# Recurrent gates on two 64-row halves of the matrix array, and a written order for the recurrence

## The chip, the cores and the metric

The kernel runs on one core of a Trainium2 chip. A core has a matrix engine (TensorE, PE in the rows; its weight loads are PEld), a vector engine (VectorE, DVE), a scalar engine (ScalarE, ACT), a general engine (GpSimd, POOL) and a queue engine that issues most DMAs (SyncE, SP). The metric is the device time of one execution in microseconds (us), the median of three runs.

## The reference

Two layers of a latent-diffusion backbone, on 256 context and 1024 latent tokens of width 1024 (T = 1280 in the kernel). The change lies in layer 0, where one projection `z = u @ w_in` feeds a bidirectional gated recurrence (16 heads of 64 channels), a Fourier mixer and a SiLU gate path. What the gates compute:

```python
xh = xc.reshape(b_, length, LRU_HEADS, LRU_HEAD_DIM)          # 16 heads x 64
g = einsum('blhi,ghij->gblhj', xh, gate_w) + gate_b           # g: recurrence gate, input gate
r = sigmoid(g[0]); i = sigmoid(g[1])
log_a = -LRU_C * r * softplus(-lam)
a = exp(log_a)
b = sqrt(-expm1(2 * log_a)) * (i * xc)                        # then h_t = a_t h_(t-1) + b_t
```

There are two directions, so four 64x64 gate matrices per head; `xc` is a depthwise convolution of width 4 of the recurrent part of z. Both scans are added and multiplied by `silu` of the gate path. The Fourier mixer takes four other groups of 128 channels of z, and layer 1 is a latent attention, which the change leaves alone.

## The kernel before, in words

Channels lie on partitions, tokens along the free axis. The projection is computed in 24 blocks of 128 output channels: `in0(m)` (lines 259 to 272) fills `z_m` in PSUM from 8 k-tiles in 3 passes (high weight by high input, high by low, low by high: an exact split of float32 in two), each pass in pieces of 512, 512 and 256 tokens. One such pass of three matmuls is called a position below; a block has 24. Blocks 0 to 7 are the recurrent channels (tile j holds heads 2j and 2j+1), 8 to 11 the Fourier groups (`fourier`, line 434), 12 to 19 the gate paths of tiles 0 to 7. Two blocks of z have room in PSUM, beside two banks (`gtile`, line 141) for everything else. The blocks run in the order z12, z0, z1, z2, z13, z3, z14, ..., z7, z18, z19, z8, z9, and so on.

`w0_load` (line 274) brings a block's weights (512 KB) and splits them: DVE makes the high part, POOL the low part (line 82), in two rotating buffers. `conv` (line 310) reads z with one ACT pass (bias) and six DVE passes (the taps, line 317), loads and splits the gate weights, and splits `xc`. The gate weights are a block-diagonal 128x128 matrix for each of the four gates of a tile. `gate_units` (line 332) makes 12 units of a tile: direction, gate and piece; each is three matmuls of 128 rows (`mm3`, lines 85 to 87) into one bank, and one ACT sigmoid over 128 partitions (line 345). `lru_chain` (line 349) is what follows on a tile: tanh and exp on ACT (354, 357), the drive on POOL (359), squares and square roots on ACT (361, 364), the DVE products (362, 367) and scans (369 to 379), the sum of directions on POOL (381), and the product with the gate path on DVE (402), whose result is written out.

The adaptive-norm weights of layer 1 and of the output gates are worked in between: `ada_units` (line 169) makes 16 units, each a load of 1 MB into the one `adaw` buffer, eight rows of matmuls of 32 columns (line 166), and a DVE addition out of PSUM (line 181).

The units are placed as small pieces of work between the k-tiles of `in0` (`spread`, line 255), so that the gates of tile j stand in z_(j+1), those of tile 7 in z19. The order on each engine is chosen by a scheduler from dependences; where a buffer must come free first, the instruction waits for it. SP issues its DMAs in one order, and one that waits holds those behind it. The Fourier stage's buffers (`ft_p`, line 411) take the place of those of the recurrence, so its first copy `fu<-z` (line 443) waits for the last product of tile 7 (line 402); block z10 needs the PSUM that this copy frees.

Of the kernel before, what the change touches and what calls it, by code (L numbers as in the profile page):

```python
# [38 lines left out]
PD = {0: 8, 1: 8}  # L39
# [15 lines left out]
def _body(ctx, tc, ap, out, dbg=None):  # L55
# [113 lines left out]
    def ada_units(src, row, nm):  # L169

        us = []
        for kt in range(KT):
            def u(kt=kt):
                w = aw_p.tile([P, 2048], F32, tag="adaw", name=f"adaw{nm}{kt}")
                load(w, src[kt])
# [6 lines left out]
            us.append(u)  # L182
# [26 lines left out]
    ada_end = {}  # L209

# [38 lines left out]
    ada_work = ada_units(ap["ada_1"], row1, "m") + [lambda: ada_mod(1, row1)]  # L249
    ada_work += ada_units(ap["ada_g"], rowg, "g") + [lambda: ada_gate(rowg)]  # L250
# [8 lines left out]
    def in0(m, work=()):  # L259
        wh, wl = ws.pop(m) if m in ws else w0_load(m)  # L260
        z = z_ps.tile([P, 1536], F32, tag="z", name=f"z{m}")
        for kt in range(KT):

            with tc.issue_after(ada_end[IA[m, kt]]) if (m, kt) in IA else ExitStack():
                for wi, ui in ((wh, uh), (wh, ul), (wl, uh)):
                    for a, n in CH3:
                        TE.matmul(z[:, a : a + n], wi[:, kt, :], ui[kt][:, a : a + n],  # L267
                                  start=(kt == 0 and ui is uh and wi is wh),
                                  stop=(kt == KT - 1 and wi is wl))
            for u in spread(work, KT, kt):  # L270
# [39 lines left out]
    def conv(j, work=()):  # L310
        z = in0(j, work)
        xc = lru.tile([P, T], F32, tag="xc", bufs=2, name=f"xc{j}")
        S.activation(out=xc, in_=z[:, :T], func=AF.Identity, scale=vv("convw", 4 * j + 1), bias=vv("convb", j))
        for k in (0, 2, 3):
            for s, e in ((0, NC), (NC, T)):
                lo, hi = max(s, s + 1 - k), min(e, e + 1 - k)
                V.scalar_tensor_tensor(out=xc[:, lo:hi], in0=z[:, lo + k - 1 : hi + k - 1],  # L317
                                       scalar=vv("convw", 4 * j + k), in1=xc[:, lo:hi], op0=ALU.mult, op1=ALU.add)
        gw = lru.tile([P, 4, P], F32, tag="gw", name=f"gw{j}")
        load(gw, ap["gw"][j])  # L320
        gh = lru.tile([P, 4, P], F32R, tag="gh", name=f"gh{j}")
        gl = lru.tile([P, 4, P], F32R, tag="gl", name=f"gl{j}")
        split(gh, gl, gw, V, G)
# [1063 lines left out]
```

## Time and profile before

| | us |
| --- | --- |
| median of three runs | 1456.05 (1453.4 to 1458.35) |
| the profiled execution's own time | 1450.71 |
| its span | 1448.9 |
| PE busy | 1402.8 (97%) |
| DVE busy | 903.4 (62%) |
| POOL busy | 678.5 (47%) |
| ACT busy | 541.3 (37%) |

The mean granted clock of the matrix engine in this execution was 0.995 of full speed. The chain of work that ended last is for 73% PE and for 17% DVE.

How to read the rows further down. A row of the timeline gives the start in us from the span's start, the duration in us, the engine, the line, the operation, its operands (out<-in, buffer numbers left out), its shapes and how many followed in a run (x3); in brackets at the end the idle time before it and what ended that. Matmuls overlap, so what one costs is read from the starts, not from the durations. A row of the windows gives the stretch, its length, then for PE, PEld, DVE, ACT and POOL the busy us with the number of instructions, then the granted clock of PE (1.00 is 2.4 GHz, 0.50 is 1.2 GHz), the mean busy share of the DMA engines, and GB/s. A row of the waits gives the waiting engine, name and line, what it waited for, then us in total, times, and the longest.

### The profile page before, as it was taken

What the parts mean: (1) busy time and instruction counts of PE and PEld (TensorE: products, weight loads), DVE (VectorE), ACT (ScalarE), POOL (GpSimd) and SP (SyncE); (2) the same over time, 40 slices, a digit from 0 to 9 for tenths busy, and PEclk for the clock granted to TensorE, in tenths of its full rate; (3) what the DMA queues carried; (4) which work ended last, traced back from release to release, by engine and by line L of the source; (5) the groups of instructions that cost most, each with busy time, mean ns of one, the idle gap of its engine ahead of it and who ended that gap; (6) DMA issues with size and microseconds to landing.
All of it is one profiled execution on the core that took longest, in us unless ns stands there. A gap on an engine that the chain in (4) does not pass through costs nothing.

```text
span 1448.9 us, 19809 instructions
## 1 busy us (share of the span) xinstructions
PE 1402.8 (97%) x7912; PEld 1005.8 (69%) x7912; DVE 903.4 (62%) x1454; ACT 541.3 (37%) x664; POOL 678.5 (47%) x314
## 2 busy tenths in 40 slices
PE   6998999999999999998999999999999999999997
PEld 3776777777788878887986665555555555555686
DVE  5659768665855343336835446657565757563798
ACT  2276666656112231103431143344434344445210
POOL 1124434444210233312241158667766876699643
PEclk9999999999999999999999999999999999999999
DMA  8713232233303473321061131011101010124342
GB/s 301 248 52 113 98 113 102 95 105 106 126 16 97 157 248 119 115 71 34 34 182 66 44 99 51 23 45 48 52 16 38 29 38 16 37 69 167 115 131 88
DMA packets 65869, 134.10 MB, mean 93 GB/s; under 512 B 5864, under 2 KB 31720, under 8 KB 63472
## 3 DMA queue, kind: packets, MB, share of 16 engines
q1 hardware_dynamic: 63328, 124.83, 26.3%
q0 software_dynamic: 2016, 7.60, 1.4%
q8 instruction: 62, 1.02, 0.3%
q10 hardware_dynamic: 432, 0.39, 0.1%
q14 instruction: 31, 0.25, 0.1%
HBM read 101.14 MB, written 24.66 MB: 87 GB/s over the span
## 4 chain that ended last, share of the span: by engine, by line
PE 73%; DVE 17%; issue 3%; DMA 3%; ACT 2%; POOL 1%; SPq 0%; DVEq 0%; POOLq 0%; ACTq 0%
PE s L1073 13%; PE z L267 11%; PE y L646 10%; PE po L1089 10%; PE mx L976 6%; PE in1g L85 2%; PE in1g L87 2%; PE in1g L86 2%; DVE xc L317 2%; PE yf L1210 2%; DVE gate L367 1%; DVE th L362 1%; DVE hf L1260 1%; DVE gate L378 1%; PE rp L1106 1%
## 5 line engine op out<-in xcount | busy, mean ns | idle before, releaser
L1079 POOL TENSOR_TENSOR ra<-ra,p 128x1024 f32<-128x1024 f32 x112 | 269.9, 2410 | 90.2 <-ACT p L1075 87.0
L978 DVE TENSOR_REDUCE m<-mx 128x1 f32<-128x512 f32 (+1 forms) x384 | 210.3, 590 | 100.4 <-PE mx L976 99.5
L1075 ACT ACTIVATE p<-s 128x1024 f32<-128x1024 f32 x160 | 163.5, 1026 | 203.9 <-PE s L1073 202.0
L267 PE MATMUL z<-uh,w0h 128*128 128x512 f32 (+1 forms) x576 | 149.8, 367 | 4.3 <-ACT uh L76 4.3
L82 POOL TENSOR_TENSOR w0l<-w,w0h 128x1024 fp32r<-128x1024 f32 x24 | 63.9, 2664 | 184.0 <-DVE w0h L78 127.8
L267 PE MATMUL z<-ul,w0h 128*128 128x512 f32 (+1 forms) x576 | 148.0, 362 | 0.0
L267 PE MATMUL z<-uh,w0l 128*128 128x512 f32 (+1 forms) x576 | 147.8, 362 | 0.0
L267 PEld LDWEIGHTS z<-uh,w0h 128*128 128x128 f32 x576 | 98.1, 190 | 33.3 <-issue 10.7
L267 PEld LDWEIGHTS z<-ul,w0h 128*128 128x128 f32 x576 | 97.0, 191 | 18.8 <-issue 1.2
L267 PEld LDWEIGHTS z<-uh,w0l 128*128 128x128 f32 x576 | 96.5, 190 | 18.4 <-issue 2.0
L1073 PE MATMUL s<-R,KR 33*128 33x512 f32 (+1 forms) x640 | 101.4, 392 | 0.0
L345 ACT ACTIVATE gate<-gps,vec 128x512 f32<-128x512 f32 (+1 forms) x96 | 57.6, 617 | 103.2 <-PE gps L87 103.1
L976 PEld LDWEIGHTS mx<-Kh,Qh 64*128 64x128 f32 x384 | 38.3, 185 | 65.3 <-DVE m L978 31.3
L976 PE MATMUL mx<-Kh,Qh 64*128 64x512 f32 (+1 forms) x384 | 81.9, 404 | 1.3 <-DVE m L978 1.3
L1089 PE MATMUL po<-p,v_even 128*64 128x512 f32 x320 | 77.5, 605 | 0.0
L1089 PE MATMUL po<-p,v_odd 128*64 128x512 f32 x320 | 77.5, 605 | 0.0
L381 POOL TENSOR_TENSOR gate<-gate,gate 128x1280 f32<-128x1280 f32 x8 | 23.9, 2992 | 112.2 <-DVE gate L378 97.1
L976 PE MATMUL mx<-KR,R 64*128 64x512 f32 (+1 forms) x384 | 71.6, 355 | 0.0
L1073 PEld LDWEIGHTS s<-R,KR 33*128 33x128 f32 (+1 forms) x640 | 61.0, 184 | 13.4
L1073 PE MATMUL s<-Qh,Kh 64*128 64x512 f32 x320 | 69.8, 431 | 0.0
L649 DVE TENSOR_TENSOR n<-gbc,y 128x1024 f32<-128x1024 f32 x10 | 12.2, 1222 | 85.7 <-PE y L646 85.7
L1114 DVE RECIPROCAL ri<-ri 128x128 f32<-128x128 f32 x64 | 59.4, 938 | 9.9 <-ACT ri L1109 9.9
(358 smaller groups left out, 3063.0 us busy)
## 6 DMA issues: line engine op xcount, KB each, us to landing
w<-in_w SPq DMA_DIRECT2D x24, 512.0 KB
adaw<-in_ada SPq DMA_DIRECT2D x32, 256.0 KB
adawm<-in_ada SPq DMA_DIRECT2D x8, 1024.0 KB
adawg<-in_ada_g SPq DMA_DIRECT2D x8, 1024.0 KB
y_dr<-sg SPq DMA_DIRECT2D x10, 640.0 KB
woraw<-in_wo SPq DMA_DIRECT2D x12, 512.0 KB
xt<-in_x_cm SPq DMA_DIRECT2D x8, 640.0 KB
yra<-y_dr SPq DMA_DIRECT2D x10, 512.0 KB
```

What stands on the lines that cost most here:

```text
L82: el.tensor_tensor(out=lo, in0=src, in1=f(hi), op=ALU.subtract)
L85: TE.matmul(o, lh, rh, start=start, stop=False)
L267: TE.matmul(z[:, a : a + n], wi[:, kt, :], ui[kt][:, a : a + n], start=(kt == 0 and ui is uh and wi is wh), stop=(kt == KT - 1 and wi is wl))
L345: S.activation(out=gt[d, g][:, a : a + n], in_=ps[:, :n], func=AF.Sigmoid, bias=vv("gateb", 4 * j + i))
L646: TE.matmul(ps[:, 512 * hf : 512 * hf + 512], a[k], b[k][:, 512 * hf : 512 * hf + 512], start=(k == 0 and a is yh and b is woh), stop=(k = ...
L976: TE.matmul(ps[a][:, :n], q[r, P * t : P * t + P], k[r, a0 : a0 + n], start=st, stop=not st)
L978: V.tensor_reduce(out=m3s[t][:, a, i : i + 1], in_=ps[a][:, :n], axis=AX.X, op=ALU.max)
L1073: TE.matmul(ps[:, a, :], k[r, ks], w[r, c], start=(j == 0), stop=(j == len(parts) - 1))
L1075: S.activation(out=es, in_=ps, func=AF.Exp, scale=SCALE)
L1079: G.tensor_tensor(out=ra, in0=st["e"][0] if kt == 1 else ra, in1=es, op=ALU.add)
L1089: TE.matmul(st["o"][64 * a : 64 * a + 64, :], quad[q][6][:, k, 128 * i + 64 * a : 128 * i + 64 * a + 64], st["e"][k][:, a, :], start=(k == ...
L1114: V.reciprocal(out=st["ri"][:, d], in_=st["ri"][:, d])
```

## The change

The gate weights are stored as 128x2x128: row halves are the two heads of the tile, and the 128 columns of a direction hold the 64 outputs of both gates. A unit is now a direction and a piece: for each of the three passes, two matmuls of 64 rows, head 0 on the upper half of the array's rows and head 1 on the lower, each into a bank of its own (line 375 of the new kernel). Its result is read by four sigmoids over 64 partitions (line 379): two heads by two gates. A tile so has 6 units of 6 matmuls and 24 sigmoids. The gate weight load shrinks from 256 to 128 KB, and its splits by half. The scans write into another buffer.

From z1 to the end of z8, PE, DVE, ACT and POOL issue what the code writes, in the order in which it is written; SP's order is still chosen. Per tile there are 48 positions (z_(j+1), then z_(13+j)), and `slots0` says what is issued after which. The blocks now run z12, z0, z1, z13, z2, z14, ..., z7, z19, z8, z9, and the gates of tile 7 stand in z8. An adaptive-norm unit stands at positions 0, 38 and 44 of each tile, and its load is issued after the unit before it.

```diff
+            def dma(kt=kt):
+                adaw[nm, kt] = aw_p.tile([P, 2048], F32, tag="adaw", name=f"adaw{nm}{kt}")
+                load(adaw[nm, kt], src[kt])
             def u(kt=kt):
-                w = aw_p.tile([P, 2048], F32, tag="adaw", name=f"adaw{nm}{kt}")
-                load(w, src[kt])
+                w = adaw.pop((nm, kt))
                 acc = gtile(f"ada{nm}{kt}")
...
-            us.append(u)
+            us.append((dma, u))
...
-    def in0(m, work=()):
+    def in0(m, work=(), at=None):
         wh, wl = ws.pop(m) if m in ws else w0_load(m)
         z = z_ps.tile([P, 1536], F32, tag="z", name=f"z{m}")
         for kt in range(KT):
             with tc.issue_after(ada_end[IA[m, kt]]) if (m, kt) in IA else ExitStack():
-                for wi, ui in ((wh, uh), (wh, ul), (wl, uh)):
+                for i, (wi, ui) in enumerate(((wh, uh), (wh, ul), (wl, uh))):
                     for a, n in CH3:
                         TE.matmul(z[:, a : a + n], wi[:, kt, :], ui[kt][:, a : a + n],
                                   start=(kt == 0 and ui is uh and wi is wh),
                                   stop=(kt == KT - 1 and wi is wl))
+                    for u in at.get(3 * kt + i, ()) if at else ():
+                        u()
...
-        gw = lru.tile([P, 4, P], F32, tag="gw", name=f"gw{j}")
...
+        gws[j] = lru.tile([P, 2, P], F32, tag="gw", name=f"gw{j}")
...
+    def gates(j, d, c):
+        def run():
+            a, n = CH3[c]
+            if c == 0:
+                for g in range(2):
+                    gt[j, d, g] = lt(f"gate{d}{g}_{j}")
+            gh, gl = gws[j]
+            xh, xl = hls[j]
+            ps = [gtile(f"gps{j}{d}{c}{h}") for h in range(2)]
+            for i, (w, x) in enumerate(((gh, xh), (gh, xl), (gl, xh))):
+                for h in range(2):
+                    r = slice(64 * h, 64 * h + 64)
+                    TE.matmul(ps[h][:, :n], w[r, d, :], x[r, a : a + n], start=(i == 0), stop=(i == 2))
+            for h in range(2):
+                for g in range(2):
+                    r = slice(64 * g, 64 * g + 64)
+                    S.activation(out=gt[j, d, g][64 * h : 64 * h + 64, a : a + n], in_=ps[h][r, :n], func=AF.Sigmoid,
+                                 bias=vv("gateb", 4 * j + 2 * h + d)[r, :])
+        return run
...
-                        mm3(ps[:, :n], gh[:, i, :], gl[:, i, :], xh[:, a : a + n], xl[:, a : a + n], True, True)
-                        S.activation(out=gt[d, g][:, a : a + n], in_=ps[:, :n], func=AF.Sigmoid, bias=vv("gateb", 4 * j + i))
...
+    order0.enter_context(tc.manual_schedule(engines={e.engine for e in (TE, V, S, G)}))
+    def ada_next():
+        if ada_work:
+            _, u = ada_work.pop(0)
+            u()
+        if ada_work and ada_work[0][0]:
+            ada_work[0][0]()
...
+        c, b = ch[j], ch.get(j - 1)
+        A, B, nxt = j + 1, 13 + j, j + 2 if j < 6 else 8
+        if j < 7:
+            put_(0, ada_next, lambda: w0_dma(nxt), lambda: gw_dma(A))
+            put_(4, lambda: w0_high(B), lambda: w0_low(B))
+        if b:
+            put_(0, b["square", 1])
+            put_(1, b["beta", 0])
+            put_(2, b["root", 0])
+            put_(3, b["beta", 1])
+            put_(4, b["root", 1])
+            put_(5, b["scaled", 0], b["scan", 0])
+            put_(6, b["scaled", 1], b["scan", 1])
+            put_(7, lambda: silu(j, 0))
+            put_(11, lambda: silu(j, 1))
+            put_(12, b["both"])
+            put_(21, b["gated"])
+        us = [gates(j, d, k) for d in range(2) for k in range(3)]
+        for p, u in zip(UNITS[0 if j == 0 else 1 if j < 7 else 2], us):
+            put_(p, u)
+        if j == 7:
+            return w
+        put_(25 if j == 0 else 21, c["drive", 0])
+        put_(24, lambda: conv_bias(A))
+        put_(25, lambda: conv_taps(A, CUTS[:2]))
+        put_(28, lambda: conv_taps(A, CUTS[2:]))
+        if j < 6:
+            put_(24, lambda: w0_dma(B + 1))
+        put_(30, lambda: w0_high(nxt), lambda: w0_low(nxt))
+        put_(35, c["drive", 1], lambda: x_split(A, 0), lambda: x_split(A, 1), lambda: gw_split(A))
+        put_(38, ada_next)
+        put_(44, ada_next)
+        put_(36, c["tanh", 0], c["tanh", 1])
+        put_(39, c["exp", 0])
+        put_(42, c["exp", 1])
+        put_(46, c["square", 0])
+        return w
+    UNITS = ((16, 21, 24, 27, 31, 34), (10, 15, 20, 23, 29, 34), (8, 12, 15, 17, 20, 23))
+    for j in range(7):
+        w = slots0(j)
+        zc[j + 1] = in0(j + 1, at={p: w[p] for p in range(24)})
+        zc[13 + j] = in0(13 + j, at={p: w[24 + p] for p in range(24)})
+    z8 = in0(8, at=slots0(7))
+    order0.close()
...
-            gw[j, s, :, s] = lru_gate_w[0].reshape(4, H, 64, 64)[:, 2 * j + h].transpose(1, 0, 2)
+    a["gw"] = lru_gate_w[0].reshape(2, 2, 8, 2, 64, 64).transpose(2, 3, 4, 0, 1, 5).reshape(8, P, 2, P)
```

On PE, one gate unit of tile 3 in block z4. In the names, `gps3000` is the gates' PSUM tile of tile 3, `xh3`, `xl3` the split input, `gh3`, `gl3` the split gate weights, `z4` the block, `uh`, `ul`, `w0h`, `w0l` its operands. Before:

```order
L267 MATMUL z4_1392<-uh0_120,w0l_4_1389 128x512 x2
L267 MATMUL z4_1392<-uh0_120,w0l_4_1389 128x256
L85 MATMUL gps3000_1403<-xh3_1267,gh3_1263 128x512
L86 MATMUL gps3000_1403<-xl3_1268,gh3_1263 128x512
L87 MATMUL gps3000_1403<-xh3_1267,gl3_1264 128x512
L267 MATMUL z4_1392<-uh1_121,w0h_4_1388 128x512 x2
L267 MATMUL z4_1392<-uh1_121,w0h_4_1388 128x256
```

And now:

```order
L270 MATMUL z4_1523<-ul3_131,w0h_4_1422 128x512 x2
L270 MATMUL z4_1523<-ul3_131,w0h_4_1422 128x256
L375 MATMUL gps3000_1588<-xh3_1454,gh3_1458 128x512
L375 MATMUL gps3001_1589<-xh3_1454,gh3_1458 128x512
L375 MATMUL gps3000_1588<-xl3_1455,gh3_1458 128x512
L375 MATMUL gps3001_1589<-xl3_1455,gh3_1458 128x512
L375 MATMUL gps3000_1588<-xh3_1454,gl3_1459 128x512
L375 MATMUL gps3001_1589<-xh3_1454,gl3_1459 128x512
L270 MATMUL z4_1523<-uh3_123,w0l_4_1423 128x512 x2
```

The unit of three matmuls into one bank is one of six into two, and stands further back in its block.

On SP, the DMAs issued around tiles 1 to 3 with what each waits for (`Pool`: POOL's semaphore, `PE`: PE's; `DMAHW`: an earlier transfer). `adawm5` is the load of the sixth adaptive-norm unit, `w0_4` the weights of block 4, `gw3` gate weights, `y_dr` a result written out. Before:

```order
L61 DMA adawm3_1089<-in_ada_1 128x2048 [waits DMAHW6_49,DMAHW1_49,PE_49]
L61 DMA y_dr_150<-sg0_522 128x1280 [waits DVE_49]
L61 DMA gw3_1261<-in_gw 128x512 [waits DMAHW0_49,Pool_49]
L61 DMA w0_4_1386<-in_w0 128x1024 [waits DMAHW5_49,Pool_49]
L61 DMA adawm4_1206<-in_ada_1 128x2048 [waits DMAHW1_49,PE_49]
L61 DMA w0_15_1578<-in_w0 128x1024 [waits DMAHW7_49,Pool_49]
L61 DMA y_dr_150<-sg1_1097 128x1280 [waits DVE_49]
L61 DMA adawm5_1373<-in_ada_1 128x2048 [waits DMAHW5_49,PE_49]
```

And now:

```order
L60 DMA adawm3_903<-in_ada_1 128x2048 [waits DMAHW1_49,DMAHW0_49,PE_49]
L60 DMA adawm4_925<-in_ada_1 128x2048 [waits DMAHW1_49,PE_49]
L60 DMA w0_15_1080<-in_w0 128x1024 [waits DMAHW5_49,Pool_49]
L60 DMA y_dr_150<-sg0_522 128x1280 [waits DVE_49]
L60 DMA w0_4_1231<-in_w0 128x1024 [waits DMAHW6_49,Pool_49]
L60 DMA adawm5_1177<-in_ada_1 128x2048 [waits DMAHW2_49,PE_49]
L60 DMA gw3_1233<-in_gw 128x256 [waits DMAHW7_49,Pool_49]
L60 DMA adawm6_1207<-in_ada_1 128x2048 [waits DMAHW6_49,PE_49]
L60 DMA adawm7_1229<-in_ada_1 128x2048 [waits DMAHW0_49,PE_49]
```

The adaptive-norm loads, which stood one by one among the others, now stand in twos and threes, and `adawm5` stands right behind `w0_4`.

On PE at the end of the stretch, where block z9 ends and the Fourier stage's first products (`dft_c`, `dft_s`, then `aps0a`, `aps0b` from the folded copy `fold`) stand. Before:

```order
L267 MATMUL z9_2877<-uh7_127,w0l_9_2874 128x512 x2
L267 MATMUL z9_2877<-uh7_127,w0l_9_2874 128x256
L440 MATMUL dft_c_2837<-fw_2738,cosd_2740 128x512
L440 MATMUL dft_s_2840<-fw_2738,sind_2741 128x512
L267 MATMUL z10_3051<-uh0_120,w0h_10_3047 128x512 x2
L267 MATMUL z10_3051<-uh0_120,w0h_10_3047 128x256
L267 MATMUL z10_3051<-ul0_128,w0h_10_3047 128x512 x2
L267 MATMUL z10_3051<-ul0_128,w0h_10_3047 128x256
L267 MATMUL z10_3051<-uh0_120,w0l_10_3048 128x512 x2
L481 MATMUL aps0a_2905<-cw_100,fold_2737 128x128 x4
```

And now:

```order
L270 MATMUL z9_2976<-uh7_127,w0l_9_2973 128x512 x2
L270 MATMUL z9_2976<-uh7_127,w0l_9_2973 128x256
L564 MATMUL dft_c_2936<-fw_2916,cosd_2918 128x512
L564 MATMUL dft_s_2939<-fw_2916,sind_2919 128x512
L605 MATMUL aps0a_3004<-cw_100,fold_2915 128x128 x4
L605 MATMUL aps0b_3022<-sw_101,fold_2915 128x128 x4
L270 MATMUL z10_3150<-uh0_120,w0h_10_3146 128x512 x2
```

The eight matmuls of z10 that stood ahead of `aps0a` stand behind it.

## Rows read from the trace of the kernel before

**Rows 1.** The windows, the stretch of the recurrence.

```profile
160.00:365.00 205.00, 200.14 (x1045) 158.81 (x1044) 147.17 (x129) 130.23 (x136) 82.32 (x31) 1.00 0.30 101
```

**Rows 2.** The timeline of PE, two positions of a block.

```profile
78.57 0.75 PE L267 MATMUL z<-uh,w0h 128*128 128x512 f32 x3
79.16 0.75 PE L267 MATMUL z<-ul,w0h 128*128 128x512 f32 x3
```

**Rows 3.** The timeline of PE in layer 1, 64-row among 128-row matmuls.

```profile
804.34 0.39 PE L87 MATMUL in1g<-u1h,wgl 128*128 128x512 f32 x1
804.66 0.49 PE L976 MATMUL mx<-Kh,Qh 64*128 64x512 f32 x2
805.00 0.40 PE L976 MATMUL mx<-KR,R 64*128 64x512 f32 x2
805.32 0.50 PE L85 MATMUL in1g<-u1h,wgh 128*128 128x512 f32 x1
805.66 0.40 PE L86 MATMUL in1g<-u1l,wgh 128*128 128x512 f32 x1
```

**Rows 4.** The waits of PE, 57 to 365 us.

```profile
PE gps L85 <- DVE adarow L181: 6.3, 3, 4.0
PE gps L85 <- DVE adarowg L181: 3.2, 3, 1.1
PE gps L85 <- DVE mod L191: 1.2, 1, 1.2
```

**Rows 5.** The timeline of PE, then of SP: an adaptive-norm unit and the next load.

```profile
228.54 1.06 PE L166 MATMUL adag<-adawg,cond 128*32 128x512 f32 x8
...
229.66 0.33 SPq L61 DMA_DIRECT2D adawg<-in_ada_g  x1
```

**Rows 6.** The windows behind that load.

```profile
231.00:234.00 3.00, 3.00 (x17) 2.56 (x16) 0.20 (x1) 1.83 (x3) 0.00 (x0) 1.00 0.83 341
234.00:237.00 3.00, 3.00 (x19) 2.56 (x18) 2.15 (x2) 3.00 (x5) 2.27 (x1) 1.00 0.00 0
```

**Rows 7.** The timeline of ACT, the gates and the chain of tile 7.

```profile
347.87 0.68 ACT L345 ACTIVATE gate<-gps,vec 128x512 f32<-128x512 f32 x1
348.44 1.35 ACT L354 ACTIVATE th<-gate,vpos 128x1280 f32<-128x1280 f32 x1
349.69 0.47 ACT L345 ACTIVATE gate<-gps,vec 128x256 f32<-128x256 f32 x1
...
351.47 1.37 ACT L357 ACTIVATE aa<-gate,vneg 128x1280 f32<-128x1280 f32 x1
357.98 2.42 ACT L361 ACTIVATE gate<-aa 128x1280 f32<-128x1280 f32 x2
```

**Rows 8.** The timeline of DVE (taps), and a group of the page (POOL's splits).

```profile
237.34 4.82 DVE L317 SCALAR_TENSOR_TENSOR xc<-z,vec,xc 128x255 f32<-128x255 f32 x6
...
L82 POOL TENSOR_TENSOR w0l<-w,w0h 128x1024 fp32r<-128x1024 f32 x24 | 63.9, 2664 | 184.0 <-DVE w0h L78 127.8
```

**Rows 9.** The timeline of PE, DVE and ACT: end of z8, of tile 7, Fourier's start.

```profile
366.85 0.39 PE L267 MATMUL z<-uh,w0h 128*128 128x512 f32 x1
...
380.93 1.02 PE L440 MATMUL dft_c<-fw,cosd 128*128 128x512 f32 x2
...
386.64 0.57 PE L481 MATMUL aps0a<-cw,fold 128*128 128x128 f32 x3 [2.21 <-DVE fold L458]
...
375.43 3.67 DVE L402 TENSOR_TENSOR sg<-sg,gate 128x1280 f32<-128x1280 f32 x1 [2.85 <-POOL gate L381]
...
379.21 1.23 ACT L443 COPY fu<-z 128x1280 f32<-128x1280 f32 x1 [15.07 <-DVE fold L459]
```

**Rows 10.** The windows at two waits of PE.

```profile
113.00:117.40 4.40, 0.38 (x3) 0.03 (x1) 4.40 (x3) 1.94 (x2) 2.38 (x1) 0.86 0.55 225
117.40:120.00 2.60, 2.60 (x8) 2.23 (x9) 2.60 (x4) 0.69 (x1) 0.00 (x0) 0.50 0.63 252
385.00:388.00 3.00, 1.36 (x12) 1.39 (x13) 3.00 (x12) 0.19 (x1) 0.00 (x0) 1.00 1.09 399
```

More of the change, by code (lines that the diff above doesn't have):

```diff
@@ L38 @@
 CUT = (0, 1)
-PD = {0: 8, 1: 8}
 ORD = "a0 w0 u0 u1 a1 w1 u2 u3 a2 u4 u5 a3 u6 u7"
@@ L209, in _body @@
     ada_end = {}
+    adaw = {}
     def ada_part(h):
@@ L272, in in0, with w0_dma, w0_high, w0_low @@
         return z
-    def w0_load(m, eh=V):
-        w = w_p.tile([P, KT, P], F32, tag="w", name=f"w0_{m}")
-        load(w, ap["w0"][m])
+    wr = {}
+    def w0_dma(m):
+        wr[m] = w_p.tile([P, KT, P], F32, tag="w", name=f"w0_{m}")
+        load(wr[m], ap["w0"][m])
+    def w0_high(m, eh=V):
         wh = w_p.tile([P, KT, P], F32R, tag="wh", name=f"w0h_{m}")
         wl = w_p.tile([P, KT, P], F32R, tag="wl", name=f"w0l_{m}")
-        split(wh, wl, w, eh, G)
-        return wh, wl
+        copy(eh, wh, wr[m])
+        ws[m] = wh, wl
+    def w0_low(m):
+        wh, wl = ws[m]
+        G.tensor_tensor(out=wl, in0=wr.pop(m), in1=f(wh), op=ALU.subtract)
+    def w0_load(m, eh=V):
+        w0_dma(m)
+        w0_high(m, eh)
+        w0_low(m)
+        return ws[m]
     ws = {}
@@ L308, in _body @@
     lru, lru_c = pool("lru", side="right")
[L310 to L318, printed above, removed]
-        gw = lru.tile([P, 4, P], F32, tag="gw", name=f"gw{j}")
[L320 to L323, printed above, removed]
-        xh = lru.tile([P, T], F32R, tag="xh", name=f"xh{j}")
-        xl = lru.tile([P, T], F32R, tag="xl", name=f"xl{j}")
-        split(xh, xl, xc, V, V)
-        return xc, gh, gl, xh, xl
+    CUTS = [(k, max(lo, lo + 1 - k), min(e, e + 1 - k)) for k in (0, 2, 3) for lo, e in ((0, NC), (NC, T))]
@@ new lines, in gw_dma, with gw_split, x_split @@
+    def gw_dma(j):
+        gws[j] = lru.tile([P, 2, P], F32, tag="gw", name=f"gw{j}")
+        load(gws[j], ap["gw"][j])
+    def gw_split(j):
+        gh = lru.tile([P, 2, P], F32R, tag="gh", name=f"gh{j}")
+        gl = lru.tile([P, 2, P], F32R, tag="gl", name=f"gl{j}")
+        split(gh, gl, gws[j], V, G)
+        gws[j] = gh, gl
+    def x_split(j, part):
+        if part == 0:
+            hls[j] = [lru.tile([P, T], F32R, tag=f"x{c}", name=f"x{c}{j}") for c in "hl"]
+            V.tensor_copy(out=hls[j][0], in_=xcs[j])
+        else:
+            V.tensor_tensor(out=hls[j][1], in0=xcs[j], in1=f(hls[j][0]), op=ALU.subtract)
@@ new lines, in silu @@
+    def silu(j, part):
+        if part == 0:
+            sgs_[j] = lru.tile([P, T], F32, tag="sg", bufs=2, name=f"sg{j}")
+            S.activation(out=sgs_[j], in_=zc[12 + j][:, :T], func=AF.Sigmoid)
+        else:
+            V.tensor_tensor(out=sgs_[j], in0=sgs_[j], in1=zc[12 + j][:, :T], op=ALU.mult)
+    zc[12] = in0(12)
+    silu(0, 0)
+    silu(0, 1)
+    zc[0] = in0(0)
+    conv_bias(0)
+    conv_taps(0, CUTS)
+    gw_dma(0)
+    gw_split(0)
+    x_split(0, 0)
+    x_split(0, 1)
+    w0_load(1)
@@ new lines, in _body @@
+    UNITS = ((16, 21, 24, 27, 31, 34), (10, 15, 20, 23, 29, 34), (8, 12, 15, 17, 20, 23))
[5 more added lines that the diff above has]
+    order0.close()
+    c = ch[7]
+    for n in ("drive", "tanh", "exp", "square", "beta", "root", "scaled", "scan"):
+        for d in range(2):
+            c[n, d]()
+    c["both"]()
+    c["gated"]()
@@ L434, in fourier @@
     def fourier(g, work=()):
-        z = in0(8 + g, work)
+        z = in0(8 + g, work) if g else z8
         if g == 0:
```

136 lines of the change are left out of this document (61 added, 75 removed).

## The prediction

> **What bounds the kernel now.** I read the windows first. Over the stretch that the change touches PE is busy 200.1 of 205 us at the full clock, ACT 130, DVE 147, POOL 82 [rows 1]: PE sets the time, and what is taken from or added to its work counts in full, until another engine's chain is late. Next the waits of PE in this stretch: three entries, 6.3, 3.2 and 1.2 us, 10.7 in all, named as gate matmuls waiting for the additions of adaptive-norm units in the two PSUM banks [rows 4]; those additions waited for loads. Last the timeline at the end of the stretch, where the recurrence hands over to the Fourier stage: z8 ends at 366.85, z9 and the two small transforms run beside the last tile's chain, and PE waits only 2.2 us for the folded copy [rows 9]. So before, work of PE covers that chain nearly to its end.
>
> **The gates themselves.** Consecutive positions start .59 apart [rows 2], for 1280 columns, so a 512-column matmul takes .235 and a 256-column one .117. A tile's gates before: 8 units of 3 x .235 and 4 of 3 x .117, 7.05 us. Now 6 units a tile. The nearest rows for two 64-row matmuls among 128-row ones are in layer 1 [rows 3]: from the start at 804.34 to that at 805.66 stand a 128-row matmul, two pairs of 64-row ones and a 128-row one, four slots of .235, .94, and they take 1.32. Two pairs start .34 + .32 apart where the halves one after another would take .94: the halves do run side by side, and leaving and re-entering the 128-row form costs about .38 in all. A unit then costs 3 x .235 + .38 = 1.09, or .73 for 256 columns; a tile 4 x 1.09 + 2 x .73 = 5.82. Gain 1.23 x 8 tiles: **-9.8**. Bounds: if the change of form cost nothing, -28.2; if the halves ran one after another with that price, +18 more than before.
>
> The Trainium skill speaks to this place on both sides, in "TensorEngine Tiling (Array Packing)": its section Theoretical Speedup gives up to 2x for a contraction of 64 or less, by which alone this term would be -28.2; its section Key Properties says that changing the tiling mode drains the engine. The trace agrees with the second, .38 for an excursion [rows 3].
>
> **The adaptive-norm loads.** The 10.7 us of waits go, since the units stand elsewhere. What is late next: a unit's 8 matmuls take 1.06, and the next load, with one buffer, is issued 1.12 after the unit's start [rows 5]. Its traffic is over by 234.0 [rows 6], 4.3 us at most after the issue at 229.66. So two units can't start closer than about 5.4. From position 44 to position 0 of the next tile PE has 1.06 + 4 x .587 = 3.4: it waits 2.0, in four tiles (the 18 pieces of work, mod and gate among them, last for six tiles; where the pair is broken by those two, no load is needed): 8. From 38 to 44 it has 1.06 + 6 x .587 = 4.6, a wait of .85 if the load leaves at once. But SP holds it behind the next block's weights, which wait for POOL's low split (the place shown in the order, `adawm5` behind `w0_4`). That split is reached from the end of z through sigmoids queued on ACT (4 x .57 = 2.3), the bias pass (1.3) [rows 7], the taps (4.8), the high part (about 1, my estimate from the low part's 2.66) and the low part (2.66) [rows 8]: 12.1 us, then the 512 KB of weights go ahead of or beside the load, half its bytes. PE is through the unit at position 38 after 15 x .587 + 1.8 of gates + 1.06 = 11.7. So the load leaves some .4 late and lands 1.3 later for the shared traffic: a wait of 2.5, in three tiles, 7.5; in tile 0, where the load stands behind gate weights that wait for POOL's second drive, I take 4.5. Together 20, less 10.7: **+9.3**. Bounds: none of these waits, -10.7; each 2 us longer, +25.
>
> **ACT's sigmoids.** A 64-partition sigmoid isn't in the trace. The nearest row is the 128-partition one, .57 for 512 columns from start to start [rows 7], and I take the same, since the columns are as many; half of that is the lower bound. A unit then holds ACT for 2.3 (1.4 for 256 columns), and both banks with it, while PE comes back to the gates after three positions (1.76) at five places in tiles 0 and 7: .5 each, 2.5. In z8 the sigmoids also queue behind what is left of tile 6 on ACT (a square, two roots, a SiLU pass at about 1.25 and two or three table loads of 1.3, some 8 us from the block's start [rows 7]), where the first unit's results are ready at 5.8: another 2.5. **+5**; bounds 0 and, with ACT late in every tile, +40. In tiles 1 to 6 the gaps are five positions behind 512-column units: hidden. ACT would then have some 30 us of work in a tile of 37.
>
> **The end of the stretch.** Before, the last sigmoid of tile 7 ends at 350.16, during z19, and `aps0a` starts at 386.64: 36.5 [rows 7, 9], with z8, z9 and two transforms to cover it. Now tile 7's gates stand in z8, one block later, and only z9 (366.85 to 380.93, 14.1) and the transforms (1.0) come before `aps0a`, for z10 needs the PSUM that the copy frees. The chain itself: 36.5, less some 4 in which the SiLU pass of tile 7 stood in it (the first exp ends about 352.7, a second would end at 354, the squares start at 357.98), plus 1.25 for a tanh that now follows the last sigmoid, 33.7; from the last gate matmul to the last sigmoid's end 1.5. So the last gate matmul to `aps0a` takes 35, where the end of z8 to `aps0a` took 386.64 - 366.85 = 19.8: **+15**. Bounds: +12 if nothing else of the Fourier setup delays the chain (no excess in the 33.7 taken from a shared stretch), +19 if the 4 us don't go.
>
> **The clock.** In the wait of 4.4 at 113 the granted clock falls to the lower level and stays there for some us of work behind it (.86, then .50); in a stretch with 1.6 us of idle time at 385 it stays at 1.00 [rows 10]. So waits of 2 to 4 us can cost about as much again, or nothing. Before lost some 5 us so by its two longest waits (an estimate from the windows at .50). Eight waits of 2 to 4.5 and an idle time of some 17 us at the end, of which I charge half: **+4**, bounds -5 and +15.
>
> The rest (smaller gate splits on DVE and POOL, 128 KB less per gate load, the scan's other buffer) lies on engines with room, beside PE's matmuls: 0; if DVE were late, it would show in the terms above.
>
> **Sum.** -9.8 + 9.3 + 5 + 15 + 4 = +23.5 on the profiled execution's 1450.7, or 1474.2. The median shown is 5.35 higher: 1479.6, say 1480.
>
> **Rivals.**
> First, the loads land in time. If a load lands within 3.4 us of PE's release of the buffer and isn't held behind the block's weights, PE doesn't wait in the pairs, no clock falls, and the term is -10.7 with -5 of clock; with -9.8, 5 and 15: -5.5, 1450.5. For it: the traffic row shows the queues at .83, most bytes between 231 and 234 [rows 6], so it may land before 233.5. Against it: that needs 3.4, and the order has the weights ahead. If the end of the chain is shorter too, it is well faster.
> Second, the change of form costs nothing when the same pairs come six in a row: -28.2 in place of -9.8 gives +5.1, 1461. For it: inside the excursion the pairs start .33 apart in a place where other waits may hide [rows 3]; against it: the same rows.
> Third, ACT becomes the bound: if a sigmoid of 64 partitions took visibly longer than .57, or its four in a row hold the banks for longer, the units of all tiles wait for it: about 1 us for each of 40 units, 1500.
> Fourth, the end is covered after all (the copy doesn't wait for tile 7's product, or z10 goes ahead): 15 less, 1465.
>
> **How the numbers follow.** Main case .52 (1480, its own range 1465 to 1498); loads in time .17 (1450); free change of form .10 (1461); ACT bound .07 (1500); covered end .09 (1465); free change and loads in time together .05 (1432). A measurement of this kernel tells a change from none at about .3%, 4.4 us. Faster: the loads in time mostly, and the .05: .21. Within .3%: shares of the two cases near 1450 to 1461: .09. Slower: .70. The range from 1446 to 1498 leaves out the last case and the upper tail.
>
> **What would show it.** Gate pairs (64x512) starting .235 apart within a unit and a unit taking about 1.1; if .7, the second rival. Waits of PE named for `adawm` and `adawg` loads, eight of 2 to 4.5 us; if they are missing, the first. Sigmoids of 64 partitions at .57, 24 a tile; PE waiting on ACT in z8. A gap of 15 us or more before `aps0a`, put down to the fold. A granted clock of .5 in stretches behind those gaps. I am wrong if the end of z8 comes earlier than 366.85, or if PE doesn't stand still ahead of `aps0a`.

## The result, and the profile after

The changed kernel takes 1500.94 us (median of four, 1499.07 to 1506.19) where the kernel before took 1456.85 beside it: a ratio of 1.031, 95% interval 1.028 to 1.035. That is 44 us slower; 23.5 were forecast, and the time lies just past the range, which ended at 1498. The profiled execution after, 1506.19, is the slowest of its four, and the one before, 1450.71, is below its four: of the 55 us between the two profiles 11 come from that.

From 57 us to the first matmul of the output projection the stretch grew from 437.6 to 479.6 us, by 42.0. I split it by summing over PE's records and the clock's: idle time 14.9 before and 49.8 now, +34.9; time at the lower clock 10.2 and 51.2, of which PE worked in 9.0 and 34.5, and at half the clock half of that is lost, 4.5 and 17.2, +12.7; what is left is PE's work as it would be at the full clock, 418.2 and 412.5, -5.7.

The windows after, of the stretch of [rows 1], with the same columns:

```profile
160.00:365.00 205.00, 190.26 (x989) 140.97 (x988) 172.48 (x126) 155.42 (x185) 86.00 (x31) 0.97 0.25 90
```

PE is busy 190 us of 205 where it was 200, at a mean clock of .97. Its waits after, from 57 to 460 us, which answer to [rows 4]:

```profile
PE adam L165 <- DMA adawm<-in_ada: 11.9, 4, 5.4
PE adag L165 <- DMA adawg<-in_ada_g: 11.8, 4, 4.4
PE dft_c L564 <- DMA cosd<-in_cosd: 11.8, 1, 11.8
PE gps L375 <- ACT gate L379: 6.2, 6, 4.1
PE aps0a L605 <- DVE fold L582: 4.4, 1, 4.4
PE adatr L190 <- DVE adarow L183: 2.7, 1, 2.7
```

Eight waits for loads (four of 4.1 to 5.4 us at position 44, four of .6 to 1.9 at position 0), the sigmoids in z8, and 16.2 us ahead of the Fourier stage: the forecast's places. The timeline of PE after, around one gate unit of z8 at the full clock, answers to [rows 2, 3]:

```profile
365.75 0.74 PE L270 MATMUL z<-uh,w0l 128*128 128x512 f32 x3
366.42 0.50 PE L375 MATMUL gps<-xh,gh 64*128 64x512 f32 x2
366.76 0.39 PE L375 MATMUL gps<-xl,gh 64*128 64x512 f32 x2
366.99 0.40 PE L375 MATMUL gps<-xh,gl 64*128 64x512 f32 x2
367.32 0.85 PE L270 MATMUL z<-uh,w0h 128*128 128x512 f32 x3
368.01 0.74 PE L270 MATMUL z<-ul,w0h 128*128 128x512 f32 x3
```

From 365.75 to 368.01 are 2.26 us, less two positions of .587: the unit costs 1.09. Over the units of the stretch that stand whole and at the full clock the median is 1.10 for 512 columns and .75 for 256.

The timeline of ACT, then of PE, behind that unit, beside [rows 7]:

```profile
371.42 1.24 ACT L439 ACTIVATE sg<-z 128x1280 f32<-128x1280 f32 x1
372.55 2.78 ACT L379 ACTIVATE gate<-gps,vec 64x512 f32<-64x512 f32 x4
...
373.98 0.79 PE L375 MATMUL gps<-xh,gh 64*128 64x512 f32 x1 [4.08 <-ACT gate L379]
```

The unit's matmuls ended at 367.4, but ACT came to its sigmoids only at 372.55, behind two square roots, a table load and the SiLU pass of line 439. The four sigmoids start .70 us apart and hold ACT for 2.78.

The timeline after at a load, of PE, POOL and SP, beside [rows 5]:

```profile
141.39 1.06 PE L165 MATMUL adam<-adawm,cond 128*32 128x512 f32 x8
...
141.05 2.77 POOL L293 TENSOR_TENSOR w0l<-w,w0h 128x1024 fp32r<-128x1024 f32 x1 [6.93 <-DVE w0h L77]
...
143.84 0.33 SPq L60 DMA_DIRECT2D w<-in_w  x1
144.26 0.38 SPq L60 DMA_DIRECT2D adawm<-in_ada  x1
...
150.80 1.94 PE L165 MATMUL adam<-adawm,cond 128*32 128x512 f32 x8 [4.64 <-DMA adawm<-in_ada]
```

PE is through the unit at position 38 at 142.4; the next load leaves at 144.26, as soon as POOL's low split is done and the weights ahead of it are issued, and the next unit starts 6.5 us later, at the lower clock (1.94 where the one before took 1.06). The windows after show that clock, beside [rows 10]:

```profile
146.00:150.80 4.80, 0.16 (x3) 0.03 (x1) 2.69 (x2) 4.78 (x5) 2.66 (x2) 0.93 0.73 282
150.80:157.00 6.20, 6.20 (x20) 3.65 (x20) 0.69 (x1) 0.28 (x1) 0.00 (x0) 0.51 0.48 170
157.00:160.00 3.00, 2.45 (x16) 1.26 (x15) 1.13 (x2) 0.00 (x0) 0.00 (x0) 1.00 0.27 36
```

A wait of 4.6 us is followed by 6 us at .51: it costs some 3 us more than itself. Last the end of the stretch, the timeline of ACT, DVE and PE, beside [rows 9]:

```profile
413.39 0.44 ACTq L544 DMA_DIRECT2D cosd<-in_cosd  x1
...
418.24 1.49 DVE L426 TENSOR_TENSOR sg<-sg,th 128x1280 f32<-128x1280 f32 x1 [3.06 <-POOL th L420]
...
419.76 2.35 ACT L567 COPY fu<-z 128x1280 f32<-128x1280 f32 x2 [14.35 <-DVE sg L426]
...
416.18 2.04 PE L564 MATMUL dft_c<-fw,cosd 128*128 128x512 f32 x2 [11.76 <-DMA cosd<-in_cosd]
...
424.32 2.04 PE L605 MATMUL aps0a<-cw,fold 128*128 128x128 f32 x8 [4.42 <-DVE fold L582]
```

z9 is done at 404.4, and PE stands until the last tile's buffers come free: the load of `cosd` is issued only at 413.4, the copy waits for the last product, and `aps0a` starts at 424.3 where it started at 386.6.

### The profile page after: what moved, and what is told of

It is laid out like the page before. It is cut to its first block, busy times and chain, and to the rows that moved or that the text cites. A ratio compares the mean times of both kernels' runs of the same rounds, so it can differ in the third digit from the quotient of the medians.

```text
span 1504.4 us, 19960 instructions
## 1 busy us (share of the span) xinstructions
PE 1416.8 (94%) x7912; PEld 993.6 (66%) x7912; DVE 944.1 (63%) x1454; ACT 597.2 (40%) x756; POOL 684.0 (45%) x314
## 4 chain that ended last, share of the span: by engine, by line
PE 62%; DVE 17%; issue 5%; DMA 4%; POOL 2%; ACT 1%; SPq 0%; DVEq 0%; POOLq 0%; ACTq 0%
PE s L1197 12%; PE y L770 10%; PE po L1213 10%; PE mx L1100 6%; PE z L270 5%; PE in1g L84 2%; PE in1g L86 2%; PE in1g L85 2%; DVE xc L339 2%; DVE hf L1384 1%; DMA adawg<-in_ada_g 1%; DVE gate L408 1%; DVE th L416 1%; POOL th L420 1%; DVE th L399 1%
## 5 line engine op out<-in xcount | busy, mean ns | idle before, releaser
L293 POOL TENSOR_TENSOR w0l<-w,w0h 128x1024 fp32r<-128x1024 f32 x24 | 69.2, 2883 | 280.5 <-DVE w0h L77 196.4
L270 PE MATMUL z<-uh,w0h 128*128 128x512 f32 (+1 forms) x576 | 154.7, 376 | 4.4 <-ACT uh L75 4.3
L270 PE MATMUL z<-ul,w0h 128*128 128x512 f32 (+1 forms) x576 | 151.2, 370 | 0.0
L379 ACT ACTIVATE gate<-gps,vec 64x512 f32<-64x512 f32 (+1 forms) x192 | 117.4, 612 | 47.1 <-PE gps L375 44.2
L1197 PE MATMUL s<-Ql,Kh 64*128 64x512 f32 x320 | 64.0, 391 | 0.0
```

Source lines behind the costliest of these rows:

```text
L293: G.tensor_tensor(out=wl, in0=wr.pop(m), in1=f(wh), op=ALU.subtract)
L379: S.activation(out=gt[j, d, g][64 * h : 64 * h + 64, a : a + n], in_=ps[h][r, :n], func=AF.Sigmoid, bias=vv("gateb", 4 * j + 2 * h + d)[r, :])
L1197: TE.matmul(ps[:, a, :], k[r, ks], w[r, c], start=(j == 0), stop=(j == len(parts) - 1))
```

## The experiments

Ratios are to the kernel before, run beside each. Theory: the row halves gain, and the written order loses more, by waits and by the clock behind them.

**e1: the adaptive-norm units at other positions.**

```diff
-        put_(38, ada_next)
-        put_(44, ada_next)
+        put_(18, ada_next)
+        put_(38, ada_next)
```

> The changed kernel with the adaptive-norm units at positions 0, 18 and 38 of a tile in place of 0, 38 and 44; nothing else differs. In the changed kernel's profile PE waits 23.7 us for these loads and runs at the lower clock behind five of the waits. Theory (the spacing of the units against one buffer is what costs, and the clock falls with the waits): the waits fall below 5 us and the five low-clock stretches between 100 and 290 us go, 28 to 36 us less, 1465 to 1473. Rival (the loads are held on SP behind block weights wherever they stand): the waits move to other positions, at most 10 us less, 1490 or more. Rival (the low clock has another cause than the waits): 20 us less, 1481, with low-clock stretches left.

1487.86 us, 1.020 [1.017, 1.023]: 13 us less than the changed kernel, where 28 to 36 were expected. The waits for loads fell from 23.7 to 6.5 us, but the gates now waited 7.7 us for additions of these units that stood in VectorE's order behind other work. Neither theory nor rival: the wait partly changed its place.

**e2: work put into the waits.** A unit that waits first runs extra matmuls into the bank that it then overwrites; 104 in all.

```diff
                 acc = gtile(f"ada{nm}{kt}")
+                for _ in range(FILL.get((nm, kt), 0)):
+                    TE.matmul(acc, uh[0][:, 0:P], uh[0][:, 0:512], start=True, stop=True)
                 ada_mm(acc, w, kt, True, True)
```

> The changed kernel with extra 512-column matmuls on PE ahead of the adaptive-norm units that wait: 18 of them at four units (position 44) and 8 at four (position 0), 104 in all, 24 us of added work at the full clock, into the bank that the unit then overwrites. No wait is removed, PE only works through them. Theory (an idle PE lowers the clock, and that costs some 9 us behind these five waits): time falls although work is added, 5 to 10 us less, 1491 to 1496. Rival (the clock is not set by those waits, or what it costs is small): no change or up to 6 us more, since the added work overshoots some of the waits.

1494.42 us, 1.025 [1.023, 1.028]: 6.5 us less, with 24 us of work added (the changed kernel's interval begins where this one ends). In the stretch idle time falls by 19.8, PE's work grows by 24.9, and the loss at the lower clock falls from 17.2 to 8.1. At the place shown above, the timeline of PE in e2, then its windows:

```profile
146.02 4.28 PE L181 MATMUL adam<-uh 128*128 128x512 f32 x18
150.23 1.06 PE L166 MATMUL adam<-adawm,cond 128*32 128x512 f32 x8
```

```profile
149.00:156.00 7.00, 6.68 (x34) 4.31 (x32) 0.69 (x1) 2.09 (x2) 0.12 (x1) 1.00 0.49 171
```

The unit starts at 150.23 instead of 150.80, but it takes 1.06 instead of 1.94 and the clock stays at 1.00. The four low stretches behind the filled waits are gone; the one behind a wait that was not filled, for the modulation's row at 193, is still there. So the low clock follows the waits, and about 9 us of the loss are its price here.

**e3: the row halves alone, in the order before.** The kernel before with the new units of line 375, half as many, and half as many empty places ahead of them in tiles 0 and 1; nothing else.

```diff
-                        mm3(ps[:, :n], gh[:, i, :], gl[:, i, :], xh[:, a : a + n], xl[:, a : a + n], True, True)
...
+                    for i, (w, x) in enumerate(((gh, xh), (gh, xl), (gl, xh))):
+                        for h in range(2):
+                            r = slice(64 * h, 64 * h + 64)
+                            TE.matmul(ps[h][:, :n], w[r, d, :], x[r, a : a + n], start=(i == 0), stop=(i == 2))
```

> The kernel before with the gates on two row halves alone (128x2x128 weights, 6 units a tile of 6 matmuls into two banks, 24 sigmoids); the scheduler's order and the adaptive-norm units as before. Forecast's theory (an excursion to 64 rows costs .38, a unit 1.09): 5 to 10 us less than before, 1447 to 1452. Rival (the changed form costs more, or the four sigmoids hold the banks so that PE waits): same as before or slower, up to 1475, with PE waiting for ACT at the gates.

1483.28 us, 1.017 [1.015, 1.019]: slower than theory or rival. In the stretch PE's work is 429.0 against 418.2, the loss at the lower clock 13.7 against 4.5, idle time 18.2 against 14.9. The timeline of PE in e3 says why the work grew:

```profile
206.02 0.39 PE L346 MATMUL gps<-xh,gh 64*128 64x256 f32 x1
206.25 0.27 PE L346 MATMUL gps<-xl,gh 64*128 64x256 f32 x1
206.36 0.28 PE L346 MATMUL gps<-xh,gl 64*128 64x256 f32 x1
206.57 0.50 PE L267 MATMUL z<-uh,w0h 128*128 128x512 f32 x1
207.00 0.38 PE L346 MATMUL gps<-xh,gh 64*128 64x256 f32 x1
```

The scheduler issued the heads apart, 40 runs of three matmuls beside 27 of six, and three of one head cost as much (median 1.10 and .75) as six of both.

**e4: the written order alone**, with 128-row gates, two banks and sigmoids to a position.

```diff
-            ps = [gtile(f"gps{j}{d}{c}{h}") for h in range(2)]
...
+            for g in range(2):
+                ps = gtile(f"gps{j}{d}{c}{g}")
+                i = 2 * d + g
+                mm3(ps[:, :n], gh[:, i, :], gl[:, i, :], xh[:, a : a + n], xl[:, a : a + n], True, True)
+                S.activation(out=gt[j, d, g][:, a : a + n], in_=ps[:, :n], func=AF.Sigmoid, bias=vv("gateb", 4 * j + i))
```

> The changed kernel's written order with the gates in the form of before (block-diagonal 128-row matmuls, one bank and one 128-partition sigmoid for a gate and piece, two of them at each unit's position). Theory (the written order carries the loss, the row halves a gain of 6 to 10): waits for loads and the idle time ahead of the Fourier stage as in the changed kernel, PE's work 6 to 10 us more, PE's waits for sigmoids up to 6 us less: 1500 to 1510. Rival (the row halves and their 24 sigmoids cause the loss): 1460 to 1475.

1510.31 us, 1.036 [1.034, 1.037]. The order by itself loses 52 us. Its loads wait 36.8 us, more than the changed kernel's 23.7, so the difference to that one isn't the gates alone.

**e5: the end's buffers in a place of their own.**

```diff
-    ft_p, ft_c = pool("ft", side="right")
-    fus = [ft_p.tile([P, T], F32, name=f"fu{i}") for i in range(2)]
+    fe_p, fe_c = pool("fe", side="right")
+    fus = [fe_p.tile([P, T], F32, name="fu0")]
...
+    dft = [fe_p.tile([P, P], F32, name=n) for n in ("cosd", "sind")]
+    ft_p, ft_c = pool("ft", side="right")
```

> The changed kernel with the first Fourier copy, its two folds' sources, the small transform's inputs (fu0, ev, od, fw, cosd, sind) in a pool of their own, placed where the adaptive-norm weights stood, so that they no longer wait for the last tile's buffers; PE's order then has z10 ahead of the first Fourier products. Theory (in the changed kernel PE stands 16.2 us ahead of the Fourier stage because these buffers come free only when tile 7 is through, and runs 17 us at the lower clock around it): 16 less of idle time, some 6 less of clock, 1477 to 1483. Rival (the fold, which still lies in a buffer of tile 7, or z11 waits in its place): at most 8 us less, 1493 or more.

1492.29 us, 1.024 [1.021, 1.028]: 8.6 us less, about the rival's size. Of the 16.2 us 2.3 are left, but the stretch shrank by 10.0 only: the Fourier products then wait for tables and for one another, which with those 2.3 makes some 5.8 us of waits between 397 and 441, and the gates wait for sigmoids 8.3 instead of 6.2.

**e6: three matmuls of head 0, then three of head 1.**

```diff
-            for i, (w, x) in enumerate(((gh, xh), (gh, xl), (gl, xh))):
-                for h in range(2):
+            for h in range(2):
+                for i, (w, x) in enumerate(((gh, xh), (gh, xl), (gl, xh))):
```

> The changed kernel with the six matmuls of a gate unit in another order: three of head 0, then three of head 1, instead of alternating. The same work and as many excursions to 64 rows. Theory (two halves run side by side only when their matmuls stand next to each other; the run with the halves alone showed three of one head costing as much as six alternating): a unit takes 6 x .235 + .38 = 1.8 for 512 columns and 1.1 for 256 instead of 1.10 and .75, 28 us more, 1522 to 1535. Rival (the array takes the second head's matmuls beside the first's anyway): no change within 5 us.

1497.92 us, 1.028 [1.025, 1.030], and a unit costs 1.11 and .75 as before: my theory fell, the rival held. The timeline of PE in e6, a unit of 256 columns:

```profile
126.42 0.40 PE L375 MATMUL gps<-xh,gh 64*128 64x256 f32 x2
126.65 0.28 PE L375 MATMUL gps<-xl,gh 64*128 64x256 f32 x2
126.76 0.28 PE L375 MATMUL gps<-xh,gl 64*128 64x256 f32 x2
```

Written three and three, the matmuls of this unit still start in pairs, the second head's first one with the first head's first. The two heads run side by side in this order too, so alternation isn't needed. What e3 lacked is the second head in the same excursion.

**e7: e3 with the six matmuls kept in order** (`tc.manual_schedule` on PE around a unit's loop).

> The kernel before with the gates on row halves as in e3, but the six matmuls of a unit kept in alternating order; the scheduler may still put other matmuls between them where the second bank isn't free. Theory (e3 lost because the scheduler issued each head's three matmuls apart, 69 excursions and no pairs): PE's work at the full clock falls from 429 back to about 415 in the stretch, 1455 to 1468. Rival (the 24 sigmoids are what costs in e3): 1478 or more, with waits for ACT.

1471.32 us, 1.009 [1.005, 1.012]: between theory and rival, 12 us less than e3, and for another reason than mine. PE's work didn't fall (431.4): in 41 units the scheduler put block matmuls between the first gate matmul and the other five, and such a lone first matmul costs .62 or .51 of its own. Idle time (13.7 for 18.2) and the clock's loss (4.3 for 13.7) fell instead.

**e8: PE alone in written order**, on top of e7's gates: `tc.manual_schedule` on PE around the loop over tiles.

> The kernel before with the gates on row halves, alternating, and PE alone in written order through the recurrence (blocks, gate units and adaptive-norm units where the kernel before writes them, each adaptive-norm unit some 12 us from the next); ACT, DVE and POOL stay with the scheduler. Theory (the row halves gain 7 to 10 us if each unit is one undivided excursion and no wait is added): 1446 to 1453. Rival (an order written for PE alone adds waits, for gates at their inputs or for sigmoids, and clock behind them): 1465 or more.

1507.36 us, 1.034 [1.031, 1.036]: the rival, and more. Gates wait 21.3 us for sigmoids in 23 waits and 14.7 for the adaptive-norm work, and 24.5 are lost at the lower clock. In e7, where the scheduler may put block matmuls past a waiting unit, the gates wait .2 us for sigmoids.

**e9: the units at 2, 13 and 36.**

```diff
-            put_(0, ada_next, lambda: w0_dma(nxt), lambda: gw_dma(A))
+            put_(0, lambda: w0_dma(nxt), lambda: gw_dma(A))
+            put_(2, ada_next)
+            put_(13, ada_next)
...
-        put_(38, ada_next)
-        put_(44, ada_next)
+        put_(36, ada_next)
```

> The changed kernel with the adaptive-norm units at positions 2, 13 and 36 of a tile: at least 11 positions from one to the next, and where VectorE's written order has no chain work ahead of the unit's addition. In e1 (0, 18, 38) loads still waited 6.5 us and the gates waited 7.7 us for the additions. Theory (the units cost by their spacing and by what stands ahead of their addition on VectorE): waits for loads and additions together fall from 26 us to under 4, low-clock stretches between 90 and 330 us go, 27 to 36 us less than the changed kernel, 1465 to 1474. Rival (the loads are held on SP behind block weights): like e1, 1484 to 1490.

1506.07 us, 1.035 [1.032, 1.038]: no gain, where both theory and rival had one. The loads come in time (1.8 us of waits), and the additions take their place: five waits of 5.4 us. The timeline of DVE in e9:

```profile
113.28 2.35 DVE L417 TENSOR_TENSOR_SCAN th<-aa,th,gate 128x1024 f32<-128x1024 f32 x1
...
120.04 1.46 DVE L441 TENSOR_TENSOR sg<-sg,z 128x1280 f32<-128x1280 f32 x1
121.42 0.68 DVE L183 TENSOR_TENSOR adarow<-adarow,adam 128x512 f32<-128x512 f32 x1
```

The unit's matmuls ran at 113.9; its addition, written behind the scans, came at 121.4, and until then it held one of the two banks that the gates at position 15 need.

**e10: e9, e5's pool, and the last SiLU later.**

```diff
-            put_(7, lambda: silu(j, 0))
-            put_(11, lambda: silu(j, 1))
+            put_(7 if j < 7 else 13, lambda: silu(j, 0))
+            put_(11 if j < 7 else 16, lambda: silu(j, 1))
```

> The changed kernel with three edits: the adaptive-norm units at 2, 13 and 36, the Fourier stage's first buffers in a pool of their own (e5), and in z8 the last gate path's SiLU at positions 13 and 16 in place of 7 and 11, behind the first sigmoids. Theory (the waits and the clock behind them are the whole loss, and the row halves gain 8): e9 less 9 for the buffers and 3 to 6 for the SiLU, 1450 to 1462, level with the kernel before or a little faster. Rival (what is left, the sigmoids in z8 and the end's chain, keeps its cost and new waits appear): 1465 to 1475.

1492.33 us, 1.024 [1.022, 1.027]: 14 less than e9, but slower than theory and rival: 27 us of waits for the additions are left.

**e11: two units in a tile, at 2 and 36.**

```diff
+        put_(2, ada_next)
+        if j == 7:
+            put_(21, ada_next)
...
-        put_(38, ada_next)
-        put_(44, ada_next)
+        put_(36, ada_next)
+        if j == 0:
+            put_(13, ada_next)
+        if j == 3:
+            put_(44, ada_next)
```

> As e10, but with only two adaptive-norm units in a tile, at positions 2 and 36 (three in tiles 0 and 3, the last in z8), where e9 and e10 showed no wait for the addition and under 1.2 us for a load; the units of the output gates begin before the small transposes, and a load is issued as soon as the one buffer is free. In e10 PE waits 27 us for the additions at position 13 and runs 48 us at the lower clock behind them. Theory: these waits and the clock behind them go, 27 and some 13 us: 1450 to 1458, level with or faster than the kernel before. Rival (the written order has other waits behind these, on sigmoids or block weights, that come out once they are gone): 1465 to 1480.

1452.86 us, .996 [.994, .998]: level with the kernel before or just faster, 48 us less than the changed kernel, as the theory had it. Idle time in the stretch is 14.4 us, lower-clock loss 2.4.

**e12: e11 with 128-row gates**, by e4's edit.

> e11 with the gates in the form of before (128-row matmuls, one bank and one 128-partition sigmoid each, two at a unit's position). With the loads' waits gone, the difference to e11 is the gates' alone. Theory (unit prices in the profiles: 1.38 and .71 against 1.10 and .75, 1.07 a tile): 8 to 10 us more than e11, less up to 4 of PE's waits for sigmoids. Rival (the sigmoids cost as much as the matmuls gain): within 3 us of e11.

1440.14 us, .988 [.986, .990]: the fastest of all, 12.7 us less than e11, and against my theory in sign. The windows of the same stretch, in e11, then in e12:

```profile
160.00:365.00 205.00, 199.00 (x1057) 146.80 (x1056) 179.17 (x130) 173.52 (x206) 93.25 (x33) 1.00 0.28 99
```

```profile
160.00:365.00 205.00, 203.75 (x1062) 163.34 (x1061) 188.24 (x135) 133.49 (x143) 95.43 (x33) 1.00 0.29 101
```

And a group by line in e11, then in e12 (operands, count, busy us, mean ns, idle before):

```profile
L380 ACT ACTIVATE gate<-gps,vec 64x512 f32<-64x512 f32 x128 | 87.5, 684 | 32.5 <-PE gps L376 30.7
```

```profile
L376 ACT ACTIVATE gate<-gps,vec 128x512 f32<-128x512 f32 x64 | 42.8, 689 | 62.1 <-PE gps L86 62.1
```

In the stretch the halves take 4.5 us off PE's work (412.6 against 417.1) and bring 9.2 more of idle time (14.4 against 5.2) and .7 more at the lower clock: e11 is 5.3 longer there. ACT is busy 173 of 205 us instead of 133, since a sigmoid over 64 partitions takes as long as one over 128 and there are twice as many. But only 3.3 us of e11's idle time are waits for sigmoids, in tile 0 and in z8; e12 has none. Another 4.7 are waits for adaptive-norm loads, of which e12 has none either, and 4.3 stand ahead of `aps0a` for 2.4. In the middle tiles the halves do gain: block z7 starts at 287.48 in e11 and at 289.35 in e12. e11 loses this lead at the next load (2.2 us), in z8 and ahead of `aps0a`. That ACT's longer work also causes the waits for loads and at the end isn't shown.

The two profiles stand 17.9 us apart, 5 more than the medians. Of that 10.8 lie past the stretch, up to the last matmul, in code that both have: 5.1 of idle time, which begins with 2.9 us of waiting for `woh` on ACT for e12's .5, and 4.6 at the lower clock. Whether the halves cause it isn't settled.

## Why the prediction was wrong

The sign and the places were right; the sum came to 23.5 where the stretch grew by 42.0, because three terms were too good: the clock by 8.7 us, the loads by 6.4 and the gates by 4.1.

- **The gates**, -9.8: the unit prices came true (1.10 and .75 for 1.09 and .73), 1.04 a tile or -8.3 in all by the measured 1.38 and .71 of a pair of 128-row units. But four units of tile 7 were split by z9's matmuls, some .55 each, 2.2 in all, and PE's work fell by 5.7 in the whole. The Trainium skill's "drains" ("TensorEngine Tiling (Array Packing)", Key Properties) agrees with the .38 of an excursion; its "up to 2x" (Theoretical Speedup) is the case in which a unit would take .70, which no run shows.
- **The loads**, +9.3: PE waits 23.7 for them and 2.7 for the row that the modulation needs, 26.4 less the old 10.7: +15.7. The mechanism was as forecast, a load behind the block's weights behind POOL's split. The four waits at position 44 come to 18.6 where 12 were forecast, those at position 0 to 5.2 where 8 were. At the load shown, mis-sized were its delay (1.8 us after PE's release instead of .4) and the landing behind the weights (6.5 us instead of 5.6). POOL's split ended there 13.2 us after the block instead of 12.1: the four sigmoids took 2.8 instead of 2.3, and VectorE was still in the product of line 426 when the taps could have begun.
- **ACT's sigmoids**, +5: 6.2 us of waits, of which 4.7 in z8. The sum was near, its price was not: the prediction took .57 from one sigmoid to the next and 2.3 for four, and they take .70 and 2.8. ACT came to z8's first unit 11.5 us after the block's start, not 8.
- **The end**, +15: 16.2 us ahead of `aps0a` for the 2.2 before, +14. I named the copy's buffer; the first wait, 11.8, was for `cosd`, which lies in the same space. With that space elsewhere (e5) 2.3 are left.
- **The clock**, +4: this is the step that failed most. The loss at the lower clock is 17.2 for 4.5, +12.7. I took the two rows at 113 and 385 us as costing "as much again, or nothing" and charged half, then set the eight waits against the two of before. The profile after decides it: the four load waits of 4.1 to 5.4 us were each followed by the lower clock, the four of .6 to 1.9 were not. The wait of 2.7 for the modulation's row, the one of 4.1 in z8 and the idle time at the end were followed by it too. The four long load waits, 18.6 us, cost 9.0 more in this way, and e2 gets about 9 back by filling the waits.
- **The rest**, 0: past the stretch, up to the last matmul, the profile after is 10.4 us longer than the one before (3.7 idle, 4.9 at the clock). The other profiles spread there from 944.6 to 955.9 us, and this one has 956.2, so I don't charge it to the change; that the change has no part in it isn't shown.

One reading was wrong without hurting the sum. The prediction says that the additions that PE waited for before "waited for loads". The timelines of PE and DVE before, at the longest of these waits:

```profile
110.21 1.07 PE L166 MATMUL adam<-adawm,cond 128*32 128x512 f32 x8
...
112.55 4.18 DVE L402 TENSOR_TENSOR sg<-sg,gate 128x1280 f32<-128x1280 f32 x1 [1.56 <-POOL gate L381]
116.65 0.67 DVE L181 TENSOR_TENSOR adarow<-adarow,adam 128x512 f32<-128x512 f32 x1
```

The load had landed and the unit was through at 111.3; its addition stood behind the product of line 402 on VectorE and kept the bank, and PE's next gate matmul started at 117.38, 4.02 late. This is the wait that came back in e1 and e9 when the units were moved. (The trace has one more wait, 1.0 for `xl`, beside the 10.7.)

Of the rivals, loads in time was wrong (eight waits), the free change of form was wrong (.38), the covered end was wrong. ACT as the bound had its condition fulfilled (.70 for .57) but not its consequence: PE waits 6.2 us for sigmoids, not about 1 us at each of 40 units. That would by the prediction's own sum have given some 1515, not the 1500 it names, and that the measured time lies at 1500 is chance. Still there was something in it: with the other waits gone, the 128-row gates are the faster ones (e11, e12), though only a part of that is shown to be waits for sigmoids.

## What to carry to other kernels

When all engines get a written order, follow each PSUM bank and each single buffer through every engine that releases it: a load, an addition on VectorE or a sigmoid that stands behind other work there comes back as idle time on PE, and moving the waiting instruction can just change which queue it waits for (e1, e9), until its place suits all of them (e11). Add about half to PE's waits of some 4 to 5 us for the lower clock behind them (9.0 us behind 18.6 here). And price both ends of a matmul change: two half-height matmuls side by side saved PE 4.5 us here, but their results took twice as many sigmoids, 40 us more of ACT's time in 205, and the kernel with 128-row gates was 12.7 us faster.

## What the runs showed of the hardware that I had not expected

- Two row halves run side by side whether their matmuls alternate or come three and three (1.10 and 1.11 for the unit): it is enough that no 128-row matmul stands between. Written three and three, the first matmuls of the two heads start together in the unit shown of e6. Three of one half alone cost 1.10 as well.
- A lone 64-row matmul of 512 columns among 128-row ones costs .62, of 256 columns .51.
- Added work made the kernel faster: 104 matmuls inside waits, 6.5 us less (e2), of which the profiles show 9 at the clock and 20 of idle time, against 25 of work.
- A sigmoid reading 64 partitions and 512 columns takes .684 us, one reading 128 partitions .689. The four of a unit start .70 us apart.
